# Low weight parts by accumulating transfer in a third of the up-projection chunks

## The chip, the core and the metric

The kernel runs on one core of one Trainium2 chip. The metric is the time of one execution on the device, in microseconds (us). The core has a matrix engine (TensorE, in the profile PE for its matmuls and PEld for its weight loads), a vector engine (VectorE, DVE), a scalar engine (ScalarE, ACT), a general engine (GpSimd, POOL) and an engine that issues transfers (SyncE, SP). Each works through its own queue in order, and the queues meet at semaphores. Sixteen DMA engines move data between the device's memory and the on-chip memory SBUF; matmul results go to PSUM.

## The reference

The computation is a trunk of two layers over 256 tokens of 2048 channels, in float32. Each layer has a token mixer and a gated channel mixer, each between two RMS norms and added to the residual:

```python
for i in range(DEPTH):
    h = rms_norm(x, p['mix_pre'])
    m = mixer_dilated_gqa(h, ...) if i % 2 == 0 else mixer_mla(h, ...)
    x = x + rms_norm(m, p['mix_post'])
    h = rms_norm(x, p['ffn_pre'])
    x = x + rms_norm(conv_glu(h, *p['ffn']), p['ffn_post'])

def conv_glu(h, w_up, conv_w, conv_b, w_down):
    u = h @ w_up                                   # 2048 x 11264
    gate, val = u[..., :D_FF], u[..., D_FF:]       # D_FF = 5632
    gate = depthwise_conv3(gate, conv_w, conv_b)
    return (gelu(gate) * val) @ w_down             # 5632 x 2048
```

The product `h @ w_up`, once per layer, is the up projection of this document.

## The kernel before

All weights are read from the device's memory once, in float32, as a single list of chunks of 128 x 1024 numbers (512 KB), in the order in which the matmuls use them. Four buffers named `raw` hold what has been loaded. The matmuls need float32 numbers in two parts: a high part `whi`, which is the weight rounded to the matrix engine's float32r type, and a low part `wlo`, what the rounding left over. I call making the two parts "parting" a chunk. `_split` does it: ScalarE casts `raw` to `whi` (line L173), then VectorE subtracts `whi` from `raw` into `wlo` (L174). There are three buffers of each part. Activations are parted in the same way (`xhl`, `gh`, `gl`).

`weights()` (L187) is called for every chunk just before its matmuls. It parts chunks up to two ahead of the one in use, so that three are parted at a time, and issues loads up to five ahead from SP's queue (L156). In the passages between the sub-layers (`lead` is set) it parts one ahead only.

An up projection has 22 groups of 512 columns, gate groups and value groups in turn; a group has 8 chunks, so a layer has 176. `proj_t` works through one group: the weights are the stationary operand, each chunk has 8 blocks of 128 x 128, and each block takes two matmuls, the high part against high and low activations (512 columns, L244) and the low part against the high activations (256 columns, L245). Four PSUM banks collect the group. Then ScalarE copies half of each bank (L305), VectorE adds the halves (L306), and the gate goes through convolution and GELU, the value through the product with the gate. The PSUM banks alternate between two sets, so the next group's matmuls run meanwhile.

The down projection, the mixers' projections and the output projections draw on the same list of chunks and the same buffers. In the down projection some chunks are sums of others (class `Seven`), made on VectorE.

The program gives each engine's instructions through a tile framework that puts each engine's queue in order when the program is built. The order isn't just that of the code: in the trace the cast of a later chunk stands between two copies of one evacuation. POOL issues nothing in this kernel.

Of the kernel before, what the change touches and what calls it, by code (L numbers as in the profile page):

```python
# [9 lines left out]
F32 = mybir.dt.float32  # L10
F32R = mybir.dt.float32r
BF16 = mybir.dt.bfloat16
AF = mybir.ActivationFunctionType
ALU = mybir.AluOpType
AX = mybir.AxisListType

P = 128
# [5 lines left out]
NFG = DFF // 512  # L23
HD = 128
EPS = 1e-6
NEG = -1e30
HOLD = 3
LAGS = 3, 2, 1

XM = 0, 1, 3, 2  # L30
# [7 lines left out]
def down_order(h):  # L38

    plain = [("plain", p, o) for o in range(2) for p in range(PAIRS, KF // 2)]  # L40
    out, plain = plain[:LEAD[h]], deque(plain[LEAD[h]:])
    for p in range(PAIRS):
        for j in (0, None, None, 1, None, 2, 3, None):
            out.append(plain.popleft() if j is None else ("seven", p, j))
    return out + list(plain)


class Seven:
# [5 lines left out]
    def __init__(self, a, b):  # L54
        self.srcs, self.raw = (a, b), None
# [31 lines left out]
class Model:  # L87
# [60 lines left out]
    def _load(self, i):  # L148
        if i >= len(self.chunks) or i in self.loaded or i < self.at or i in self.made:
            return  # L150
        if isinstance(self.chunks[i], tuple):
            self.chunks[i][0].load(self)
            self.loaded[i] = None
            return
        raw = self.wp.tile([P, 1024], F32, tag="raw", name="raw", bufs=4)
        self.nc.sync.dma_start(out=raw, in_=self.chunks[i])  # L156
        self.loaded[i] = raw

    def _split(self, i, parts=1):
        if i >= len(self.chunks) or i in self.made:  # L160
            return
        self._load(i)
        raw = self.loaded.pop(i)
        seven, step = self.chunks[i] if raw is None else (None, 0)
        if seven:
            raw = seven.step(self, step)
        hi = self.wp.tile([P, 1024], F32R, tag="whi", name="whi", bufs=3)
        lo = self.wp.tile([P, 1024], F32R, tag="wlo", name="wlo", bufs=3)
        n = raw.shape[-1] // parts
        with self.behind(self.gate):  # L170
            for j in range(parts):
                s = slice(n * j, n * j + n)
                self.nc.scalar.copy(hi[:, s], raw[:, s])  # L173
                self.nc.vector.tensor_tensor(out=lo[:, s], in0=raw[:, s], in1=hi[:, s].bitcast(F32),  # L174
                                             op=ALU.subtract)
        if seven and step == 0:
            seven.sums(self)
        self.made[i] = (hi, lo)
# [8 lines left out]
    def weights(self, upto=None):  # L187

        i = self.at
        if upto is None:  # L190
            upto = i + (2 if self.lead else 3)
            self.follow()
        for j in range(i, upto):
            self._split(j)
        for j in range(upto, i + 6):
            self._load(j) if j < upto + 4 else None
        self.at += 1
        return self.made.pop(i)
# [191 lines left out]
    def out_proj(self, nk, parts, post, pre, m3, order=None, before={}):  # L390
# [27 lines left out]
        part = self.three(ss)  # L418
        ps = self.proj_tok(nk, parts, order, hold=HOLD)
        m.append(room.tile([P, 2, 512], F32, tag=tag, name="m3", bufs=bufs))  # L420
# [103 lines left out]
    def attend(self, scores, sc, mask, v, v_gen, put, sp):  # L524
# [31 lines left out]
        for i in range(2):  # L556
            nc.vector.tensor_scalar(out=p[:, i, :], in0=p[:, i, :], scalar1=den[:, i:i + 1], scalar2=None,
                                    op0=ALU.mult)
        for _ in range(LAGS[0]):
            yield  # L560
# [9 lines left out]
        use["p"] -= 1  # L570
        for _ in range(LAGS[1]):
            yield
# [28 lines left out]
    def turned(self, sp, ps, n, block, tab, put, scale=None):  # L601
# [4 lines left out]
        for t in range(2):  # L606
# [25 lines left out]
            yield  # L632
        for _ in range(LAGS[2]):
            yield
# [367 lines left out]
    def down(self, gh, gl, post, pre):  # L1002
# [75 lines left out]
        ended = None  # L1078
        for h in range(2):
            items = down_order(h)  # L1080
            units = [n for n, item in enumerate(items) if item[0] == "seven"]
            if h == 0:
                gains.append(self.gain_row(post, 1))
            n = len(items) - (HOLD if h else 0)
            todo = [(i, t) for i in range(n) for t in range(2)] + \
# [9 lines left out]
            def products(i, t, w):  # L1095
                group = []
                while used and used[0][1][:2] == (i, t):
                    q, (_, _, b, x, blk) = used.popleft()
                    group.append((banks[b], *x(), slice(512 * blk, 512 * blk + 512), q == first[b], q == last[b]))
                for bank, xh, xl, c, start, _ in group:  # L1100
                    mm(bank, xh, w[0][:, c], start=start, stop=False)  # L1101
                    mm(bank, xl, w[0][:, c], start=False, stop=False)  # L1102
                for bank, xh, _, c, _, stop in group:
                    mm(bank, xh, w[1][:, c], start=False, stop=stop)  # L1104
# [22 lines left out]
        part = self.three(ss)  # L1127
        ws = [self.weights(self.at + HOLD - j) for j in range(HOLD)]
        for t in range(2):
            for j in range(HOLD):  # L1130
                products(n + j, t, ws[j])
# [24 lines left out]
    def all_chunks(self):  # L1156
        a = self.a
        groups = lambda w, gs: [w[g, c] for g in gs for c in range(w.shape[1])]
        out = groups(a["w_in0"], [8, 6, 7, 0, 2, 4, 1, 3, 5])
        out += [a["w_out0"][g, c] for g in range(4) for c in (4, 5, 6, 7, 0, 1, 2, 3)]  # L1160

        def down(w):
            items = []
            for h in range(2):
                pairs = [Seven(w[2 * h, p], w[2 * h + 1, p]) for p in range(PAIRS)]
                items += [w[2 * h + j, p] if kind == "plain" else (pairs[p], j) for kind, p, j in down_order(h)]
            return items

        ffn = lambda l: groups(a[f"w_up{l}"], [g for j in range(NFG) for g in (j, NFG + j)]) + \
            down(a[f"w_down{l}"])  # L1170
        out += ffn(0)
        out += groups(a["w_in1"], [0, 1]) + [a["w_kr"]]
        for p in range(8):
            out += groups(a["w_qr"], [p // 4]) if p % 4 == 0 else []
            out += [a["w_qn"][p], a["w_kn"][p]]
            out += groups(a["w_v"], [p // 2]) if p % 2 == 0 else []
        out += groups(a["w_out1"], range(4))
        out += ffn(1)
        return out
# [67 lines left out]
```

## Time and profile before

| | |
|---|---|
| time, median of 2 runs | 2062.1 us (2062.04 to 2062.15) |
| span of the profiled execution | 2060.1 us |
| time outside the span (median less span) | 2.0 us |
| PE, PEld, DVE, ACT, POOL busy | 99%, 85%, 72%, 55%, 0% of the span |
| first up projection | 331 to 820 us |
| second up projection | 1326 to 1818 us |
| moved in all | 385.96 MB, 187 GB/s on average |

The profiled execution has no time of its own on record beside its span; the 2.0 us is what the median of the timed runs has more.

In rows of groups, a line reads: line of the kernel, engine, operation, output and inputs with their shapes, count, then busy time in us and the mean of one in ns, then the idle time of the engine just before them and what ended it. In rows of waits: who waited, for whom, us in total, times, the longest. In rows of stretches: from and to in us, length, busy time of PE, PEld, DVE, ACT and POOL, the granted clock of TensorE (1.00 is full), the share of the DMA engines' time that was busy, and GB/s. In rows of a timeline: start, duration, instruction, and in brackets the idle time before. Matmuls are pipelined and their ends are modelled, so their busy times overlap.

### The profile page before, as it was taken

What the parts mean: (1) busy time and instruction counts of PE and PEld (TensorE: products, weight loads), DVE (VectorE), ACT (ScalarE), POOL (GpSimd) and SP (SyncE); (2) the same over time, 40 slices, a digit from 0 to 9 for tenths busy, and PEclk for the clock granted to TensorE, in tenths of its full rate; (3) what the DMA queues carried; (4) which work ended last, traced back from release to release, by engine and by line L of the source; (5) the groups of instructions that cost most, each with busy time, mean ns of one, the idle gap of its engine ahead of it and who ended that gap; (6) DMA issues with size and microseconds to landing.
All of it is one profiled execution on the core that took longest, in us unless ns stands there. A gap on an engine that the chain in (4) does not pass through costs nothing.

```text
span 2060.1 us, 29196 instructions
## 1 busy us (share of the span) xinstructions
PE 2043.4 (99%) x10905; PEld 1750.0 (85%) x10905; DVE 1478.4 (72%) x2263; ACT 1129.3 (55%) x1753; POOL 0.2 (0%) x4
## 2 busy tenths in 40 slices
PE   9999999999999999999999999999999999999998
PEld 7888888888888888888878998888888888888886
DVE  6877757766766767878787875676766766787877
ACT  6655546555555555555465664555555555554553
POOL 0000000000000000000000000000000000000000
PEclk9999999999999999999999999999999999999999
DMA  8545566666566666566655445566566566556664
GB/s 318 176 153 161 166 197 193 186 194 193 185 194 191 185 194 189 184 211 197 203 179 170 124 134 173 176 210 189 185 193 193 184 195 193 185 184 205 204 206 141
DMA packets 108717, 385.96 MB, mean 187 GB/s; under 512 B 12064, under 2 KB 12576, under 8 KB 108576
## 3 DMA queue, kind: packets, MB, share of 16 engines
q1 hardware_dynamic: 108288, 383.83, 59.3%
q8 instruction: 85, 1.39, 0.3%
q14 instruction: 56, 0.46, 0.1%
q10 hardware_dynamic: 288, 0.28, 0.0%
HBM read 381.96 MB, written 2.10 MB: 186 GB/s over the span
## 4 chain that ended last, share of the span: by engine, by line
PE 96%; DVE 3%; issue 0%; ACT 0%; DMA 0%; DVEq 0%; SPq 0%; ACTq 0%
PE ps L244 31%; PE ps L245 16%; PE ps L230 8%; PE ps L231 8%; PE ps L232 8%; PE ps L1104 7%; PE ps L1101 7%; PE ps L1102 7%; PE ps L537 1%; PE ps L300 1%; DVE x L454 1%; DVE wlo L174 1%; PE ps L478 0%; DVE sums L1005 0%; DMA raw<-in_w_in 0%
## 5 line engine op out<-in xcount | busy, mean ns | idle before, releaser
L174 DVE TENSOR_TENSOR wlo<-raw,whi 128x1024 fp32r<-128x1024 f32 (+1 forms) x662 | 807.6, 1221 | 490.3 <-ACT whi L173 487.6
L173 ACT CAST whi<-raw 128x1024 fp32r<-128x1024 f32 (+1 forms) x662 | 694.3, 1050 | 642.7 <-PE ps L244 302.4
L244 PE MATMUL ps<-xhl,whi 128*128 128x512 f32 x2816 | 978.7, 394 | 1.0 <-DVE xhl L591 1.0
L245 PE MATMUL ps<-xhl,wlo 128*128 128x256 f32 x2816 | 779.2, 277 | 0.0
L244 PEld LDWEIGHTS ps<-xhl,whi 128*128 128x128 f32 x2816 | 527.6, 188 | 123.1 <-DVE xhl L591 2.0
L245 PEld LDWEIGHTS ps<-xhl,wlo 128*128 128x128 f32 x2816 | 528.9, 188 | 1.0 <-DVE wlo L174 0.5
L1101 PE MATMUL ps<-whi,gh 128*128 128x512 f32 x584 | 227.3, 389 | 0.0
L1102 PE MATMUL ps<-whi,gl 128*128 128x512 f32 x584 | 227.2, 389 | 0.0
L1104 PE MATMUL ps<-wlo,gh 128*128 128x512 f32 x584 | 182.0, 390 | 0.8 <-DVE wlo L174 0.8
L230 PE MATMUL ps<-whi,xhl 128*128 128x512 f32 x352 | 138.7, 395 | 0.9 <-ACT whi L173 0.8
L231 PE MATMUL ps<-wlo,xhl 128*128 128x512 f32 x352 | 137.6, 391 | 0.0
L232 PE MATMUL ps<-whi,xhl 128*128 128x512 f32 x352 | 137.2, 390 | 0.0
L1104 PEld LDWEIGHTS ps<-wlo,gh 128*128 128x128 f32 x584 | 109.1, 188 | 25.2 <-DVE wlo L174 2.7
L1101 PEld LDWEIGHTS ps<-whi,gh 128*128 128x128 f32 x584 | 109.6, 188 | 22.8
L1102 PEld LDWEIGHTS ps<-whi,gl 128*128 128x128 f32 x584 | 109.6, 188 | 22.8
L230 PE MATMUL ps<-whi,oh 128*128 128x512 f32 x256 | 100.0, 390 | 0.0
L231 PE MATMUL ps<-wlo,oh 128*128 128x512 f32 x256 | 99.7, 389 | 0.0
L232 PE MATMUL ps<-whi,ol 128*128 128x512 f32 x256 | 99.6, 389 | 0.0
L305 ACT COPY half<-ps 128x256 f32<-128x256 f32 x176 | 65.1, 370 | 43.9 <-PE ps L244 34.6
L230 PEld LDWEIGHTS ps<-whi,xhl 128*128 128x128 f32 x352 | 66.0, 188 | 14.5 <-ACT whi L173 1.1
L232 PEld LDWEIGHTS ps<-whi,xhl 128*128 128x128 f32 x352 | 66.1, 188 | 13.9
L231 PEld LDWEIGHTS ps<-wlo,xhl 128*128 128x128 f32 x352 | 66.3, 188 | 13.4 <-DVE wlo L174 0.9
(211 smaller groups left out, 2061.0 us busy)
## 6 DMA issues: line engine op xcount, KB each, us to landing
raw<-in_w_up SPq DMA_DIRECT2D x352, 512.0 KB, 4.1
raw<-in_w_down SPq DMA_DIRECT2D x128, 512.0 KB, 3.9
raw<-in_w_in SPq DMA_DIRECT2D x88, 512.0 KB, 3.7
raw<-in_w_out SPq DMA_DIRECT2D x64, 512.0 KB, 4.1
seven_a<-in_w_down SPq DMA_DIRECT2D x24, 512.0 KB, 4.5
seven_b<-in_w_down SPq DMA_DIRECT2D x24, 512.0 KB, 4.2
gb<-in_post SPq DMA_DIRECT2D x16, 256.0 KB, 3.8
raw<-in_w_qn SPq DMA_DIRECT2D x8, 512.0 KB, 3.6
```

The lines of the kernel that those rows point to most:

```text
L173: self.nc.scalar.copy(hi[:, s], raw[:, s])
L174: self.nc.vector.tensor_tensor(out=lo[:, s], in0=raw[:, s], in1=hi[:, s].bitcast(F32), op=ALU.subtract)
L230: mm(ps, lh, rh, start=start, stop=False)
L231: mm(ps, lh, rl, start=False, stop=False)
L232: mm(ps, ll, rh, start=False, stop=stop)
L244: mm(out[i], hi[:, s], x(k), start=k == 0, stop=False)
L245: mm(out[i][:, :T], lo[:, s], x(k)[:, :T], start=False, stop=k == nk - 1)
L300: self.tc.keep_in_program_order(self.nc.tensor.transpose(out, x, self.ident))
L305: self.nc.scalar.copy(b, ps[:, T:])
L1101: mm(bank, xh, w[0][:, c], start=start, stop=False)
L1102: mm(bank, xl, w[0][:, c], start=False, stop=False)
L1104: mm(bank, xh, w[1][:, c], start=False, stop=stop)
```

## The change

Three things change.

First, in both up projections every third chunk from number 8 of the layer on (8, 11, 14, ...) is wrapped in a new class `Summed`. For such a chunk ScalarE casts `raw` to `whi` as before and then also writes the negated high part into `wlo`. VectorE does nothing. A transfer issued from POOL's queue reads the same 512 KB of weights from the device's memory a second time and adds them, on the way, to what lies in `wlo`: the low part is weight minus high part, as before. All other chunks are parted as before.

Second, `whi` and `wlo` get four buffers instead of three, and `weights()` parts up to three chunks ahead instead of two, for all chunks of the kernel. Loads still reach up to five ahead.

Third, the scratch memory that the program reserves in SBUF for the descriptors of transfers issued from POOL is set to 1024 bytes per partition.

```diff
+AHEAD = 4
+class Summed:
+    def __init__(self, src):
+        self.src = src
     def _load(self, i):
         raw = self.wp.tile([P, 1024], F32, tag="raw", name="raw", bufs=4)
-        self.nc.sync.dma_start(out=raw, in_=self.chunks[i])
+        src = self.chunks[i]
+        self.nc.sync.dma_start(out=raw, in_=src.src if isinstance(src, Summed) else src)
     def _split(self, i, parts=1):
-        hi = self.wp.tile([P, 1024], F32R, tag="whi", name="whi", bufs=3)
-        lo = self.wp.tile([P, 1024], F32R, tag="wlo", name="wlo", bufs=3)
+        hi = self.wp.tile([P, 1024], F32R, tag="whi", name="whi", bufs=AHEAD)
+        lo = self.wp.tile([P, 1024], F32R, tag="wlo", name="wlo", bufs=AHEAD)
         n = raw.shape[-1] // parts
+        if isinstance(self.chunks[i], Summed):
+            with self.behind(self.gate):
+                self.nc.scalar.copy(hi, raw)
+                self.nc.scalar.activation(lo, hi.bitcast(F32), AF.Copy, scale=-1.0)
+            self.nc.gpsimd.dma_start(out=lo, in_=self.chunks[i].src, accum_op=ALU.add)
+            self.made[i] = (hi, lo)
+            return
     def weights(self, upto=None):
-            upto = i + (2 if self.lead else 3)
+            upto = i + (2 if self.lead else AHEAD)
...
-        ffn = lambda l: groups(a[f"w_up{l}"], [g for j in range(NFG) for g in (j, NFG + j)]) + \
-            down(a[f"w_down{l}"])
+        def up(w):
+            items = groups(w, [g for j in range(NFG) for g in (j, NFG + j)])
+            return [Summed(src) if i % 3 == 2 and i >= 8 else src for i, src in enumerate(items)]
+        ffn = lambda l: up(a[f"w_up{l}"]) + down(a[f"w_down{l}"])
...
-    nc = bacc.Bacc("TRN2", target_bir_lowering=False, num_devices=1)
+    nc = bacc.Bacc("TRN2", target_bir_lowering=False, num_devices=1,
+                   dynamic_dma_scratch_size=1024)
```

## The prediction

> **What bounds the kernel now.** I read the busy times first, then the chain of work that ended last, then who waited for whom inside the up projections, where the change acts.
>
> ```profile
> PE 2043.4 (99%) x10905; PEld 1750.0 (85%) x10905; DVE 1478.4 (72%) x2263; ACT 1129.3 (55%) x1753; POOL 0.2 (0%) x4
> ...
> PE 96%; DVE 3%; issue 0%; ACT 0%; DMA 0%; DVEq 0%; SPq 0%; ACTq 0%
> ```
>
> TensorE is busy for 2043.4 of 2060.1 us and makes up 96% of the chain. So 16.7 us, 0.8% of the span, is all that any change to other engines could win if TensorE's work stays as it is. POOL does next to nothing. The stages of the change come next (start and end in us; then busy time of PE, PEld, DVE, ACT and POOL, granted clock, DMA share, GB/s): the two up projections, and a third row from the kernel's start, where transfers run as fast as they ever do here.
>
> ```profile
> 331.00:820.00 489.00, 488.52 (x2824) 426.88 (x2823) 340.24 (x542) 271.56 (x419) 0.00 (x0) 1.00 0.62 191
> 1326.00:1818.00 492.00, 491.51 (x2840) 429.40 (x2840) 343.12 (x548) 274.26 (x423) 0.00 (x0) 1.00 0.62 191
> ...
> 10.00:15.00 5.00, 5.00 (x22) 3.81 (x22) 4.83 (x9) 4.59 (x7) 0.00 (x0) 1.00 1.04 417
> ```
>
> In 981 us of up projection TensorE idles for 1.0 us, at full clock. VectorE works 70% of that time and ScalarE 56%, both with room. The waits of the weight loads in the first of these stages say the same: they waited for a low part (wlo) once.
>
> ```profile
> PEld ps L244 <- DVE xhl L591: 1.0, 2, 0.8
> PEld ps L245 <- DVE wlo L174: 0.2, 1, 0.2
> ```
>
> So the VectorE work that the change takes away is off the path, and its removal is worth nothing by itself. The question is whether what replaces it arrives in time. A steady stretch of ScalarE shows the beat (start, duration, then in brackets the idle time before and who ended it):
>
> ```profile
> 456.76 1.05 ACT L173 CAST whi<-raw 128x1024 fp32r<-128x1024 f32 x1 [1.46 <-PE ps L244]
> 459.53 1.05 ACT L173 CAST whi<-raw 128x1024 fp32r<-128x1024 f32 x1 [1.72 <-PE ps L244]
> 462.30 1.05 ACT L173 CAST whi<-raw 128x1024 fp32r<-128x1024 f32 x1 [1.72 <-PE ps L244]
> 465.08 1.05 ACT L173 CAST whi<-raw 128x1024 fp32r<-128x1024 f32 x1 [1.72 <-PE ps L244]
> ```
>
> One chunk of weights takes TensorE 2.77 us. Each cast waits for the end of the matmuls that free its buffer: with three buffers that is the chunk three before, and the cast has two chunks, 5.5 us, until its own chunk's matmuls start.
>
> **The change, part by part.** 176 chunks make one up projection. Those with a remainder of 2 by three from number 8 on are 8, 11, ..., 173: 56 per layer, 112 in all.
>
> *Removed from VectorE:* 112 subtractions. *Added to ScalarE:* 112 negations of 128x1024. Both prices stand in the groups:
>
> ```profile
> L174 DVE TENSOR_TENSOR wlo<-raw,whi 128x1024 fp32r<-128x1024 f32 (+1 forms) x662 | 807.6, 1221 | 490.3 <-ACT whi L173 487.6
> L173 ACT CAST whi<-raw 128x1024 fp32r<-128x1024 f32 (+1 forms) x662 | 694.3, 1050 | 642.7 <-PE ps L244 302.4
> ```
>
> VectorE loses 112 x 1.22 = 137 us, ScalarE gains 112 x 1.05 = 118 us (I price the negation as the cast: same size, both out of SBUF). On the path: 0 for both. The negation is covered by the 1.72 us in which ScalarE idles before the next cast; without that cover each would push the next cast by 1.05 us, which has a slack of 8.3 - 2.3 us.
>
> *Added transfers:* 112 of 512 KB on POOL's queue, each adding weights to what lies in SBUF. POOL has nothing else queued, so its wait for the negation holds up nobody; behind the transfer stand the 16 low-part matmuls of that chunk, and behind the first of them all of TensorE's queue, high-part matmuls of the same chunk included. No such transfer is in the trace, so I bound it by the plain loads of the same size:
>
> ```profile
> L156 SPq DMA_DIRECT2D raw<-in_w_up x171: 327/328/328, 334.9 to 807.3; - x171
> ...
> DMA to landing us min/median/max: 3.2/4.1/5.4
> ```
>
> A plain load lands 3.2 to 5.4 us after its issue, 4.1 as a rule. At 417 GB/s 512 KB take 1.26 us, so 3.2 - 1.26 = 1.94 us lie around the moving, issue included. The accumulating one must also read what is in SBUF. From below it costs no more than the quickest load, 3.2 us. From above I take the slowest load, two further passes of the bytes (the reading back, and as much again for adding or queueing), and one whole 1.94 us more for an issue by POOL: 5.4 + 2.52 + 1.94 = 9.9 us. My value is 4.1 + 1.26 + 0.5 = 5.9 us: the median load, one more pass, and an issue dearer by a quarter of the 1.94, since it is nearest to the plain load of the same bytes over the same engines.
>
> The Trainium skill, in "Collectives: The Full Stack", section "The bandwidth ceiling: the fold count and why AG ≠ RS ≠ AR", says that the add in the transfer engines costs its two source reads and no cycles of its own. "DMA: Bandwidth & Descriptors", section "Specifications", puts the first byte of a software-issued transfer at about 1 us against 0.6 us for a hardware-issued one. By these two the transfer would be estimated at 4.1 + 1.26 + 0.4 = 5.8 us and the run would come out with my forecast; no run here shows either yet.
>
> *Moved: the lead.* With four buffers the parting of a chunk starts when the chunk four before it ends and must be done three chunks later, 3 x 2.77 = 8.3 us. Cast and negation take 2.1 us, hand-overs some 0.1. That leaves 6.1 us for the transfer, against 5.9 wanted: on time with 0.2 us to spare. Let C be the whole chain, 2.2 us plus the transfer. If C exceeds 8.3, TensorE stalls; but the chain of the next such chunk, three later, starts before that stall and gains from it, so two neighbours share C - 8.3, and the mean stall is half of it.
>
> At the ends of groups ScalarE is behind, because it evacuates PSUM in between:
>
> ```profile
> 442.89 1.05 ACT L173 CAST whi<-raw 128x1024 fp32r<-128x1024 f32 x1 [1.72 <-PE ps L244]
> 443.84 0.37 ACT L305 COPY half<-ps 128x256 f32<-128x256 f32 x1
> ...
> 445.89 1.06 ACT L173 CAST whi<-raw 128x1024 fp32r<-128x1024 f32 x1
> ...
> 451.83 1.04 ACT L173 CAST whi<-raw 128x1024 fp32r<-128x1024 f32 x1
> ```
>
> By the beat these casts were due at 445.66 and 451.20, so they come 0.2 and 0.6 us late, and with another 1.05 us of ScalarE in the same stretch up to 1.6. About four chunks of sixteen lie there, 28 of the 112. Taking 0.8 us of lateness, less 0.2 spare, halved: 28 x 0.3 = 8 us. Ends: 0 (the planner moves the evacuation) and 28 x 0.8 = 22 us.
>
> *Raw loads and their queue.* They run one fewer ahead of the parting, but parting itself is one further ahead, so the horizon of six chunks stays. SP's loads wait for a raw buffer as before:
>
> ```profile
> SPq L156 <- DVE wlo L174: 1229.2, 518, 9.2
> ```
>
> A buffer comes free 2.3 us after a parting starts (cast plus subtraction), and the load into it is cast four chunks after that start: 11.1 - 2.3 - 4.1 = 4.7 us of slack before and after. For summed chunks ScalarE alone frees it, 1.2 us sooner. If an accumulating transfer pushes a load by its whole two passes, 2.5 us, it stays inside 4.7. Cost 0; without that cover a load would stall TensorE by what exceeds it.
>
> *Transfer engines.* 191 GB/s in the stage plus a third of it at two passes is 191 x (1 + 2/3) = 318 GB/s, 76% of 417. At three passes 382 (92%), at four 446, more than there is.
>
> *The fourth buffer elsewhere.* At the two passages into the up projections one parting stands in the chain, between residual additions:
>
> ```profile
> 325.53 1.41 DVE x L454 x2
> 326.94 1.14 DVE wlo L174
> ...
> 1322.17 1.14 DVE wlo L174
> ```
>
> With a free buffer it can be done before: between 0 and 2 x 1.14 = 2.3 us won; I take 2, near the upper end, since the cast of that chunk then no longer waits for the last matmuls to free its buffer. The scratch is cut from what nothing in the kernel used so far; 0.
>
> *The sum,* against the profiled execution: 2060.1 + 0 + 8 - 2 = 2066.1 us of span, and the 2.0 us that the median of 2062.1 lies above the span: 2068 us, 0.3% above before. What this kernel's measurement can tell from no change I take as 2%, 41 us.
>
> **The rivals.**
>
> *Late transfers (slower).* Mechanism: the accumulating transfer outlasts the lead. Place: the first low-part matmul of 112 chunks. It decides from a transfer of 6.1 us on, and passes 2% at a mean stall of about 0.3 us beside the 8 us of the group ends, that is from 6.7 us on. At 4.1 + 1.26 + 1.94 = 7.3 us, the full price for POOL's issue, C is 9.5 and the sum is 112 x 0.59 = 66 us, less the 2, plus 8: 2134 us. At the upper bound, 9.9 us, it is 112 x 1.9 = 213 us, 2281 us. For it: the spare of 0.2 us is far less than what I don't know of the issue and of queueing beside loads that already fill 62% of the engines' time. Against it: plain loads at that share land within 5.4 us. Chance 0.35.
>
> *Transfers become the bound (slower).* If adding costs four passes, 446 of 417 GB/s: at least 7% of 981 us, 69 us; and by latency 4.1 + 3 x 1.26 + 0.5 = 8.4 us, C = 10.6, 112 x 1.15 = 129 us with the group ends beside it: 2062 + 129 + 6 = 2197 us. For it: nothing in the trace; against it: 24% of the speed is free at two passes. Chance 0.07.
>
> *Faster by over 2%.* TensorE's 16.7 us of idling would have to vanish two and a half times over. Less work on VectorE could matter only if TensorE itself ran slower beside it, and the clock is 1.00 in these stages. 2 us from the passages: 2060. Chance 0.01.
>
> That the change doesn't do what it says I leave out: its edits name the chunks outright.
>
> **The numbers.** Forecast (on time, with small stalls at most): 0.57, own range 2057 to 2103. Late transfers 0.35, bound by transfers 0.07, faster 0.01. The predicted time is the forecast's, 2068. The range goes from 2057 (both gains, no stalls, a little below) to 2160, which takes in two thirds of the late case; left out are its upper third, 0.12, most of the 0.07 and the 0.01. Faster by over 2% 0.01, within 2% 0.57, slower 0.42.
>
> **What would show it.** The waits of L245's weight loads: some 10 us in all for the forecast, 60 and more in the name of the POOL transfer if it is late, in alternate summed chunks. The median from issue to landing of the new transfers: below 6.1 us or above. VectorE's busy time near 1341 us, ScalarE's near 1247, 58.7 MB more moved (112 x 0.524), a DMA share in the up stages between 0.75 and 0.9 (over 1.0 for the third case). The raw loads landing in under 8 us. The forecast is wrong if the transfer takes over 6.7 us, if POOL's issue alone takes over 1 us and adds to the landing time, or if the negations, by the order on ScalarE, come later than right behind their cast.

## The result and the profile after

The changed kernel takes 2175.5 us (median of 2 runs, 2172.7 to 2178.2) against 2062.1 before: a ratio of 1.053, 95% interval 1.050 to 1.057 (the two medians alone would give 1.055). It is 113 us slower by the medians, 110 by the ratio, and lies above the stated range. The profiled execution has a span of 2171.0 us, 110.9 more than before.

The page of the changed kernel: busy times, the two transfer queues (q1 is SP's, q0 the new one from POOL; packets, MB, share of the sixteen engines' span) and the chain that ended last.

```profile
PE 2076.5 (96%) x10905; PEld 1763.7 (81%) x10905; DVE 1358.6 (63%) x2151; ACT 1236.1 (57%) x1865; POOL 97.8 (5%) x116
...
q1 hardware_dynamic: 108288, 383.83, 54.5%
q0 software_dynamic: 16128, 58.73, 16.5%
...
PE 63%; issue 20%; DMA 11%; DVE 3%; POOL 2%; ACT 1%; POOLq 0%; DVEq 0%; SPq 0%; ACTq 0%
```

VectorE's busy time fell by 120 us and ScalarE's rose by 107, a little less than the 137 and 118 that were worked out: VectorE's subtractions did lose 137 us (807.6 to 670.2) and the negations do take 118.7, but the rest of VectorE's busy time rose by 17 us, and that of ScalarE fell by 12. The chain, 96% TensorE before, now runs for 11% through DMA and for a fifth through "issue", which is time in which the engine waited for nothing that the profile shows. So I read the cause from the waits. The waits of TensorE's low-part instructions are these (L260 is the old L245; L182 is the new transfer):

```profile
PEld ps L260 <- DMA wlo<-in_w_up: 101.3, 76, 3.5
PE ps L260 <- DMA wlo<-in_w_up: 77.5, 64, 3.2
```

The new transfer's own line (durations of its issue on POOL in ns, least, median, most; then its landing):

```profile
L182 POOL DMA_DIRECT2D wlo<-in_w_up x112: 862/866/1007, 351.6 to 1913.9; - x112
...
DMA to landing us min/median/max: 5.4/7.3/9.2
```

Before, these weight loads waited for a low part once in each up projection, for 0.2 and 0.3 us. Now TensorE waits for the transfers in most of the 112 summed chunks. (The two rows can't be added: a weight load's wait and its matmul's overlap.) The transfer takes POOL 0.87 us to issue and lands 7.3 us after its issue, where a plain load took 4.1. On TensorE's timeline one stall looks like this:

```profile
459.92 0.39 PE L259 MATMUL ps<-xhl,whi 128*128 128x512 f32 x1
461.58 0.39 PE L260 MATMUL ps<-xhl,wlo 128*128 128x256 f32 x1 [1.27 <-DMA wlo<-in_w_up]
461.81 0.39 PE L259 MATMUL ps<-xhl,whi 128*128 128x512 f32 x1
```

The low-part matmul should have started some 0.23 us after the high-part one, as in the blocks behind it; it started 1.66 us after it. And this is the path of the same chunk that set the time, first on ScalarE, then on POOL:

```profile
451.53 1.05 ACT L180 CAST whi<-raw 128x1024 fp32r<-128x1024 f32 x1 [1.72 <-PE ps L259]
452.61 1.06 ACT L181 ACTIVATE wlo<-whi 128x1024 fp32r<-128x1024 f32 x1
```

```profile
454.07 0.88 POOL L182 DMA_DIRECT2D wlo<-in_w_up  x1 [8.45 <-ACT wlo L181]
```

From the start of the cast to POOL's issue are 2.54 us, and a transfer lands 7.3 us after that in the median: a chain of 9.8 us against a lead of 8.3.

### The profile page after: what moved, and what is told of

It is laid out like the page before. It is cut to its first block, busy times and chain, and to the rows that moved or that the text cites. A ratio compares the mean times of both kernels' runs of the same rounds, so it can differ in the third digit from the quotient of the medians.

```text
span 2171.0 us, 29553 instructions
## 1 busy us (share of the span) xinstructions
PE 2076.5 (96%) x10905; PEld 1763.7 (81%) x10905; DVE 1358.6 (63%) x2151; ACT 1236.1 (57%) x1865; POOL 97.8 (5%) x116
## 3 DMA queue, kind: packets, MB, share of 16 engines
q0 software_dynamic: 16128, 58.73, 16.5%
## 4 chain that ended last, share of the span: by engine, by line
PE 63%; issue 20%; DMA 11%; DVE 3%; POOL 2%; ACT 1%; POOLq 0%; DVEq 0%; SPq 0%; ACTq 0%
DMA wlo<-in_w_up 11%; PE ps L259 10%; PE ps L245 8%; PE ps L246 8%; PE ps L247 8%; PE ps L1116 7%; PE ps L1117 7%; PE ps L1119 7%; PE ps L260 6%; POOL wlo L182 2%; PE ps L552 1%; PE ps L315 1%; DVE wlo L189 1%; DVE x L469 1%; DMA raw<-in_w_up 0%
## 5 line engine op out<-in xcount | busy, mean ns | idle before, releaser
L189 DVE TENSOR_TENSOR wlo<-raw,whi 128x1024 fp32r<-128x1024 f32 (+1 forms) x550 | 670.2, 1221 | 618.1 <-ACT whi L188 615.2
L259 PE MATMUL ps<-xhl,whi 128*128 128x512 f32 x2816 | 995.9, 397 | 1.7 <-DVE xhl L606 1.7
L260 PE MATMUL ps<-xhl,wlo 128*128 128x256 f32 x2816 | 800.0, 284 | 77.9 <-DMA wlo<-in_w_up 77.5
L188 ACT CAST whi<-raw 128x1024 fp32r<-128x1024 f32 (+1 forms) x550 | 574.3, 1050 | 495.2 <-PE ps L259 250.8
L260 PEld LDWEIGHTS ps<-xhl,wlo 128*128 128x128 f32 x2816 | 535.3, 190 | 102.0 <-DMA wlo<-in_w_up 101.3
L180 ACT CAST whi<-raw 128x1024 fp32r<-128x1024 f32 x112 | 117.4, 1049 | 130.3 <-PE ps L259 127.3
L182 POOL DMA_DIRECT2D wlo<-in_w_up x112 | 97.6, 872 | 1816.7 <-ACT xhl L605 538.7
L245 PE MATMUL ps<-whi,xhl 128*128 128x512 f32 x352 | 138.8, 396 | 1.4 <-ACT whi L188 1.1
L181 ACT ACTIVATE wlo<-whi 128x1024 fp32r<-128x1024 f32 x112 | 118.7, 1060 | 2.2
L188 ACT CAST whi<-seven_a 128x1024 fp32r<-128x1024 f32 x48 | 50.6, 1054 | 103.1 <-PE ps L1117 86.4
L245 PE MATMUL ps<-whi,oh 128*128 128x512 f32 x256 | 100.0, 390 | 0.0
```

The costliest lines, as they stand in the source:

```text
L181: self.nc.scalar.activation(lo, hi.bitcast(F32), AF.Copy, scale=-1.0)
L182: self.nc.gpsimd.dma_start(out=lo, in_=self.chunks[i].src, accum_op=ALU.add)
L245: mm(ps, lh, rh, start=start, stop=False)
L259: mm(out[i], hi[:, s], x(k), start=k == 0, stop=False)
L260: mm(out[i][:, :T], lo[:, s], x(k)[:, :T], start=False, stop=k == nk - 1)
```

## The experiments

Two theories stood against each other after the result. **A, late transfers:** each transfer outlasts the lead, and what counts is the length of the chain against the lead. **B, taken speed:** 58.7 MB more through the engines, at double cost, slow everything, and what counts is the bytes. Ratios are to the kernel before on the same chip, with 95% intervals. The runs of the kernel before lie at 2062, 2071 or 2080 us, in steps of 9, so differences under half a per cent are left to the intervals.

**One chunk more of lead** (`lead_four`).

```diff
-AHEAD = 4
+AHEAD = 5
```

> The changed kernel with five buffers of each part and parting four chunks ahead; all else as changed. Theory A (late transfers): the chain of a summed chunk, cast, negation, hand-over and transfer, is 1.05 + 1.06 + 0.4 + 7.3 = 9.8 us in the changed kernel's profile, against a lead of 3 x 2.77 = 8.3. With 4 x 2.77 = 11.1 us of lead it fits but for the slowest (the longest landing is 9.2 us, chain 11.7), so nearly all of the 113 us go: 2062 to 2072 us. Theory B (the transfers take speed from everything: two passes of a third of the weights, contention with the loads): the bytes are the same, so the time stays above 2150 us.

Ratio 1.005 (1.003 to 1.008); the profiled execution takes 2071.5 us, the median of ten runs is 2078.6, which is a little above the 2062 to 2072 expected. The transfers are as slow as before; they only start a chunk earlier (landing, then TensorE's waits):

```profile
DMA to landing us min/median/max: 5.3/7.3/10.2
```

```profile
PEld ps L260 <- DMA wlo<-in_w_up: 6.2, 9, 1.7
PE ps L260 <- DMA wlo<-in_w_up: 3.7, 5, 1.4
```

Same bytes, same landing, and some 100 of the 110 us are gone. B is refuted as the main cause, A holds.

**One chunk less of lead** (`lead_two`): `AHEAD = 3`.

> The changed kernel with three buffers of each part as before, parting two chunks ahead; the third of the chunks still gets its low part by transfer. Theory A: the lead is 2 x 2.77 = 5.5 us, the chain 9.8 to 10.3, and the parting of the next summed chunk starts only after the stall of this one, so nothing is shared: 4.3 to 4.8 us of stall at each of 112 chunks, 480 to 540 us more than before, 2540 to 2600 us. Theory B: same bytes, same time as changed, about 2175 us.

Ratio 1.190 (1.186 to 1.194), 2461.5 us: 391 us more than before by the ratio, not 480 to 540. All 112 weight loads wait, up to 4.9 us.

```profile
PEld ps L260 <- DMA wlo<-in_w_up: 318.3, 112, 4.9
```

The span and the mean granted clock of the core:

```profile
core 0: 2461.5 us, clock 0.960
```

The expectation took 7.3 us for the landing. Here TensorE stands still for so long that fewer plain loads move beside the transfer: while one moves, 42 packets of plain loads start in the median, where 124 do in the changed kernel. It lands in 5.7 us: chain 2.5 + 5.7 = 8.2, less 5.5 of lead, 112 x 2.7 = 302 us. The rest is in the second row: the mean granted clock fell from 0.998 to 0.960, and by estimate that is 0.038 x 2461 = 94 us. Together 396.

**Half as many transfers** (`sixth`).

```diff
-            return [Summed(src) if i % 3 == 2 and i >= 8 else src for i, src in enumerate(items)]
+            return [Summed(src) if i % 6 == 2 and i >= 8 else src for i, src in enumerate(items)]
```

> The changed kernel with every sixth chunk summed (8, 14, 20, ...) instead of every third: 56 transfers instead of 112. Theory A with shared stalls: neighbours six apart no longer overlap, so each stalls for the whole of chain less lead, 1.5 to 2.0 us, instead of half of it: 56 x 1.5 to 2.0 = 84 to 112 us, so 2146 to 2174 us, little less than with twice as many transfers. Theory A without sharing: half of 113 us, 2119 us. Theory B: half the extra bytes, half the loss or less, at most 2119 us.

Ratio 1.035 (1.030 to 1.040): about 72 us for 56 transfers, 1.29 us each, where the changed kernel pays 110 us for 112, 0.98 each. Halving the transfers doesn't halve the loss (55 us), so neighbours three chunks apart do share a stall. The waits say the same:

```profile
PEld ps L260 <- DMA wlo<-in_w_up: 73.0, 51, 2.3
```

Here 51 of 56 weight loads wait, in the changed kernel 76 of 112. Over the first nine summed chunks of the changed kernel TensorE's timeline has low-part matmuls late by 2.4, 0, 0, 1.8, 0, 1.6, 0, 2.2 and 0 us: a late chunk is mostly followed by one on time. With sharing in full the sixth would have lost 84 us or more by the expectation, and 56 x (2.54 + 7.2 - 3 x 2.77) = 80 us by its own landing. It lost some 72, below the expected range, and the changed kernel more than half of a full stall for each chunk. So sharing is there, and somewhat weaker than the formula says.

**The negation ahead of the cast** (`neg_first`).

```diff
-                self.nc.scalar.copy(hi, raw)
-                self.nc.scalar.activation(lo, hi.bitcast(F32), AF.Copy, scale=-1.0)
+                self.nc.scalar.activation(lo, raw, AF.Copy, scale=-1.0)
+                self.nc.scalar.copy(hi, raw)
```

> The changed kernel with the two ScalarE instructions of a summed chunk exchanged: the negation is made from the raw weights, rounded in the same way, ahead of the cast. The transfer can then be issued 1.05 us sooner. Theory A: chain shorter by 1.05 us, mean stall shorter by half of it, 112 x 0.53 = 59 us: 2116 us. Theory B: 2175 us, nothing moves. Without sharing: 1.0 us off each stall, near 2062 us.

Ratio 1.064 (1.061 to 1.068): slower than the changed kernel, a miss. ScalarE's timeline shows that the edit didn't do what I wanted. The order of the queue was set when the program was built, and it put the cast first all the same in 92 of the 112 chunks:

```profile
446.83 1.05 ACT L181 CAST whi<-raw 128x1024 fp32r<-128x1024 f32 x1 [1.77 <-PE ps L259]
447.79 1.05 ACT L180 ACTIVATE wlo<-raw 128x1024 fp32r<-128x1024 f32 x1
```

So it says nothing on the length of the chain. But it is worse than the changed kernel, by more than 20 us, and it lands in 7.8 us instead of 7.3. Why, the next runs show.

**The negation on VectorE, beside the cast** (`neg_vector`).

```diff
+                self.nc.vector.tensor_scalar(out=lo, in0=raw, scalar1=-1.0, scalar2=None, op0=ALU.mult)
                 self.nc.scalar.copy(hi, raw)
-                self.nc.scalar.activation(lo, hi.bitcast(F32), AF.Copy, scale=-1.0)
```

> The changed kernel with the negation made by VectorE straight from the raw weights, beside ScalarE's cast. VectorE idles for 1.5 us before each parting in the steady stretches. Theory A: the chain is the negation (0.6 to 1.2 us, no row yet) and 7.7 us, 8.3 to 8.9, so stalls of 0 to 0.3 us on average and some at the ends of groups: 2065 to 2105 us. Theory B: 2175 us. A third possibility is that VectorE's work holds up POOL's issue, which would show as an issue longer than 0.87 us.

Ratio 1.053 (1.045 to 1.061): nothing gained, though the negation takes 0.69 us on VectorE and POOL issues 1.2 us after the cast's start instead of 2.54. POOL's issue is still 0.87 us, so the third possibility falls. The landing ate the gain:

```profile
DMA to landing us min/median/max: 7.1/8.0/9.8
```

The packets of the queues in the trace say where. Medians in us, worked out from each transfer's first and last packet and from the last issue of a load by SP before it; the third column is the sum of the first two:

```
kernel            after SP's load   issue to 1st packet   load's issue to 1st packet   1st to last   landing
changed                1.47               1.65                      3.1                  5.2          7.3
lead_two               1.47               1.61                      3.1                  3.7          5.7
no_add                 1.47               1.66                      3.1                  2.9          4.9
neg_first              0.38               2.54                      2.9                  4.9          7.8
half_columns           0.32               2.64                      3.0                  2.9          5.9
neg_vector             0.15               3.00                      3.2                  4.6          8.0
neg_vector_hold        0.15               3.03                      3.2                  4.6          8.1
```

With SP's load 1.4 us or more ahead, the first packet comes 1.6 to 1.7 us after POOL's issue. With the load less than 0.4 us ahead, in the last four rows, it comes 2.5 to 3.0 us after it, which is again some 3 us after the load's issue. In the kernel before, a load that is alone starts to move 1.0 us after its issue and has moved after about 3.2. So the transfer seems to start behind that load (theory C), and the load is one that the parting itself sets off, by freeing a raw buffer.

**Holding the raw buffer back** (`neg_vector_hold`): ScalarE reads the raw weights once more, in two halves, into a scrap tile, behind the transfer's issue.

```diff
             self.nc.gpsimd.dma_start(out=lo, in_=self.chunks[i].src, accum_op=ALU.add)
+            junk = self.small.tile([P, 512], BF16, tag="junk", name="junk", bufs=1)
+            for s in (slice(0, 512), slice(512, 1024)):
+                self.nc.scalar.copy(junk, raw[:, s])
```

> As neg_vector (negation on VectorE beside the cast), and ScalarE reads the raw weights of a summed chunk once more behind the cast, into a scrap tile that nobody uses, so that the raw buffer comes free some 1.2 us later and the plain load that waits for it is issued after the accumulating transfer instead of just before it. In neg_vector the chain was 1.3 us shorter than changed up to the issue, but the transfer's first packet came 3.0 us after its issue instead of 1.65 and nothing was won. Theory C (the transfer starts behind the load that its own cast releases): first packet back to about 1.7 us, landing about 6.7 to 7.0 instead of 8.0, chain 8.0 to 8.3 against a lead of 8.3: stalls only at the ends of groups, 2070 to 2105 us. Rival D (an early issue is slow for another reason, VectorE's work beside POOL's, say): landing stays at 8.0 us, 2165 to 2185 us.

Ratio 1.061 (1.055 to 1.066), inconclusive: SP still issued a load 0.15 us before each transfer, as the table shows, so the load that I meant to move hadn't moved. It doesn't decide between C and rival D of its expectation, by which the early issue is slow for another reason, such as VectorE's work beside POOL's.

**That load behind the transfer, in POOL's queue** (`neg_vector_pool_load`), on top of `neg_vector`:

```diff
-        self.nc.sync.dma_start(out=raw, in_=src.src if isinstance(src, Summed) else src)
+        queue = self.nc.gpsimd if i > 3 and isinstance(self.chunks[i - 4], Summed) else self.nc.sync
+        queue.dma_start(out=raw, in_=src.src if isinstance(src, Summed) else src)
```

> As neg_vector, and the plain load into the raw buffer that a summed chunk frees (the chunk four later) is issued from POOL's queue instead of SP's, where it stands behind that chunk's accumulating transfer. In neg_vector SP issued a load 0.15 us before each accumulating transfer, whose first packet then came 3.0 us after its issue; in the kernels where the last load lay 1.47 us back it came after 1.65 us. Theory C (the transfer starts only when the load issued just before it has moved): first packet back to 1.6 to 1.8 us, landing at most 7.0 us instead of 8.0, chain 1.2 + 7.0 = 8.2 us against a lead of 8.3, stalls at the ends of groups alone: 2068 to 2105 us. Rival D (VectorE's negation beside POOL's issue, or the early issue as such, delays it): first packet stays at 3.0 us, 2165 to 2190 us.

Ratio 1.014 (1.007 to 1.020), 2093.6 us, within what C expected. The first packet is back at 1.58 us after the issue, SP's last load lies 1.68 us back, and the landing is the shortest of all kernels that move 512 KB by adding beside a running TensorE:

```profile
DMA to landing us min/median/max: 5.2/6.3/7.9
```

```profile
PEld ps L261 <- DMA wlo<-in_w_up: 23.6, 38, 1.6
PE ps L261 <- DMA wlo<-in_w_up: 11.7, 25, 1.3
```

VectorE's negation and the early issue are as in `neg_vector`, so D falls. C holds, and A with it: the chain is now 1.2 + 6.3 = 7.5 us, under the lead, and the waits shrink to a quarter or less.

**Writing without adding** (`no_add`).

```diff
-            self.nc.gpsimd.dma_start(out=lo, in_=self.chunks[i].src, accum_op=ALU.add)
+            self.nc.gpsimd.dma_start(out=lo, in_=self.chunks[i].src)
```

> The changed kernel with the same transfers from POOL's queue, at the same places, that only write the weights into the low part and add nothing (the low part is then the whole weight, so the products differ from the reference). It removes the reading back of what lies in the buffer and keeps POOL's issue, the change of type and the hand-over. If the second read is what made the transfer dear: busy time of the transfers' packets from 16.5% of the engines' span to about 8 to 9%, landing from 7.3 to about 5.7 us, chain 8.2 us, stalls nearly gone: 2065 to 2085 us. If POOL's issue or the change of type is: landing stays near 7 us, time above 2150 us.

Ratio 1.006 (1.003 to 1.008). Its rows, packets of both queues, POOL's issue, the landing and TensorE's waits:

```profile
q1 hardware_dynamic: 108288, 383.83, 57.4%
q0 software_dynamic: 16128, 58.73, 9.0%
```

```profile
L182 POOL DMA_DIRECT2D wlo<-in_w_up x112: 527/530/662, 352.4 to 1818.6; - x112
...
DMA to landing us min/median/max: 4.0/4.9/6.3
...
PEld ps L260 <- DMA wlo<-in_w_up: 1.8, 4, 0.6
```

Same bytes, same queue, same change of type: without the adding the packets take 9.0% of the engines' span instead of 16.5%. A single packet of 4 KB takes 174 ns instead of 328 (medians; 159 on SP's queue). The landing falls by 2.4 us, and the stalls are gone. Of the 2.4 us 2.3 lie between the first packet and the last (5.2 and 2.9 in the table); that POOL's issue is shorter by 0.34 us doesn't bring the first packet forward. The Trainium skill, "Collectives: The Full Stack", section "The bandwidth ceiling: the fold count and why AG ≠ RS ≠ AR", puts the price of an add at two source reads; the 328 against 174 ns agree with that.

**Half the columns by transfer** (`half_columns`): in a summed chunk, VectorE subtracts the first 512 columns, and negation and transfer cover the other 512.

```diff
-                self.nc.scalar.activation(lo, hi.bitcast(F32), AF.Copy, scale=-1.0)
-            self.nc.gpsimd.dma_start(out=lo, in_=self.chunks[i].src, accum_op=ALU.add)
+                self.nc.scalar.activation(lo[:, 512:], hi[:, 512:].bitcast(F32), AF.Copy, scale=-1.0)
+                self.nc.vector.tensor_tensor(out=lo[:, :512], in0=raw[:, :512], in1=hi[:, :512].bitcast(F32),
+                                             op=ALU.subtract)
+            self.nc.gpsimd.dma_start(out=lo[:, 512:], in_=self.chunks[i].src[:, 512:], accum_op=ALU.add)
```

> The changed kernel, but in a summed chunk only the second 512 of the 1024 columns get their low part by transfer (256 KB), the first 512 by VectorE's subtraction. Theory A with a transfer that has a fixed part of about 4 us and 3.2 us for 512 KB: landing about 5.7 us, negation 0.55 instead of 1.06, chain 7.7 us, under the lead of 8.3: 2062 to 2075 us. If the transfer's time were all in its issue and completion: landing near 7 us, chain 9.0, 112 x 0.35 = 39 us, 2101 us.

Ratio 1.005 (1.003 to 1.008): as A expects (the median, 2076.6 us, is 2 us above the expected range). 256 KB land in 5.9 us, move for 2.9, and start late behind a load (2.64 us).

**Twice the scratch** (`scratch_2k`): 2048 bytes instead of 1024.

> The changed kernel with 2048 instead of 1024 bytes of scratch per partition for the descriptors of POOL's transfers. If the small scratch made POOL or the transfer engines wait, landing drops below 7.3 us and the time below 2150 us. If not, which the 0.87 us of every issue speaks for, it stays at 2170 to 2180 us.

Ratio 1.051 (1.045 to 1.057), landing 7.4 us: the scratch isn't what makes the transfer slow.

**The lead alone, and the scratch alone** (`lead_only`: no chunk is summed; `scratch_only`: the kernel before with 1024 bytes of scratch).

> The changed kernel without any summed chunk: four buffers of each part, parting three ahead, small scratch, all low parts made by VectorE. Prediction's term: 0 to 2.3 us won at the passages, 2059 to 2062 us. lead_four, no_add and half_columns all came out 0.5% above before without late transfers; in their profiles a pair of up-projection matmuls takes 348 to 351 ns on average instead of 347. If the transfers beside the matmuls do that, this kernel stays at 2062 us or below; if the place of the buffers or the order of the instructions does, it shows the same 0.3 to 0.5% (2068 to 2072 us).

> The kernel before with nothing changed but the scratch of 1024 bytes per partition. It moves all tiles to other places in SBUF and changes nothing else. If the place in SBUF slows the matmul pairs, it shows some of the 0.3 to 0.5%; else 2062 us as before.

Ratios 1.001 (0.999 to 1.004) and 1.001 (0.999 to 1.003). The second is from eleven of its twelve runs; the twelfth took 5292 us, and nothing on record says why. Neither part costs or wins anything that can be told. The profiled execution of `lead_only` took 2071.6 us, one step of 9 above the kernel before, without any transfer from POOL, and its pairs of up-projection matmuls take 350.1 ns on average instead of 346.9 (from start to start, longer pauses left out): 2816 x 3.2 ns = 9 us. In `lead_four`, `no_add` and `half_columns` they take 348.3 to 351.3 ns, so the half per cent of these three is at least in part the same lengthening. No version beat the kernel before.

## Why the prediction was wrong

*What bounds the kernel:* right. VectorE's 137 us were off the path, ScalarE's 118 pushed no later cast into TensorE's way (with a longer lead, in `lead_four`, they cost next to nothing), though the negation is a link of the late chain. The raw loads stayed harmless (landing 4.6 us in the median), the engines' share in the stages rose to 0.84 (0.75 to 0.9 expected), and the passages' 2 us can't be told from none.

*The mechanism of the loss:* named, as the rival with 0.35, with its place and its point of decision. Its signs came out: the waits of over 60 us in the transfer's name, a landing above 6.1 us, and late chunks that mostly alternate with punctual ones. A transfer of 7.3 us was even the example worked out there, but that this figure agrees is luck: the example got it by charging a full 1.94 us for POOL's issue, and the runs put the excess elsewhere. The forecast chose 5.9.

*The step that failed* is the price of the accumulating transfer, "the median load, one more pass, and an issue dearer by a quarter of the 1.94". The issue's 0.5 us was right: without adding, the transfer lands in 4.9 us, beside plain loads of 4.4 us in the same run. The pass was mis-sized. I took 1.26 us for it, at the rate of the fastest stretch of the kernel. It costs 7.3 - 4.9 = 2.4 us. In the packets' own time the price was about right: 128 packets over sixteen engines are 8 each, if they are spread evenly, and 8 x (328 - 174) ns = 1.2 us. But a transfer that moves for longer shares the engines with more of the plain loads. In the changed kernel the 18 transfers during which fewer than 50 packets of plain loads started moved in 3.8 us, the 57 with 120 to 200 such packets in 5.4 (medians). With the engines already busy for 0.62 of the time, the peak rate was the wrong price for the pass.

*The rival's sum* was too low as well, 2134 us at 7.3. Of the 41 us that are missing, 112 x 0.17 = 19 are the hand-over from ScalarE to POOL: cast to issue is 2.54 us, where I had 2.2. Another 7 are the clock, below. Of the remaining 15, some 7 are pairs of up-projection matmuls that take 349.4 ns instead of 346.9, away from stalls and from half clock (2816 x 2.5 ns). What is left lies in the ends of groups and a sharing weaker than half; I haven't separated them.

*Halving by neighbours:* it was borne out in kind (0.98 us each against 1.29 each alone), not in full.

*The range* ended at 2160 because it left out the upper third of the late case. With 2.4 us for the pass the transfer would have come to 7.0 us, and the prediction's own formula to 112 x 0.45 = 50 us: 2118 us, in the late case, and still short of what was measured.

One reading was wrong without effect: a chunk has 8 low-part matmuls, not 16, and no term was worked out from that.

## What to carry to other kernels

Before moving work from an engine that isn't on the path to a transfer, hold the whole chain against the lead: every hand-over, the issue, the moving at the share that the engines already carry, and what is issued just ahead. Here VectorE's work wasn't on the path, so taking it away won nothing, and the transfer that replaced it could only cost. One more buffer of lead won the time back nearly whole (110 us to some 10), while shortening one link (`neg_vector`) only moved the wait into the next.

## What the runs showed of the hardware

**Waiting costs clock.** TensorE's clock is granted in stretches: the changed kernel has five at half speed, each one or two times 3.41 us long or at the end of the run, where the kernel before has only the one at its end. One of them, and the stretches before and after it (granted clock third from the right):

```profile
551.20:554.60 3.40, 1.64 (x9) 1.28 (x9) 0.23 (x1) 1.59 (x3) 0.00 (x0) 1.00 0.98 329
554.60:558.00 3.40, 3.40 (x13) 2.81 (x12) 2.34 (x6) 2.59 (x7) 0.89 (x1) 0.50 0.66 175
558.00:561.40 3.40, 3.40 (x21) 3.02 (x20) 3.35 (x7) 2.79 (x5) 0.00 (x0) 1.00 0.64 120
```

In the first, TensorE was busy for 1.64 of 3.40 us; in the second it got half its clock though it had work throughout. The four stretches at half speed within the changed kernel's run came each after a stretch of 3.41 us in which TensorE was busy for 0.16, 0.35, 0.39 and 0.48 of the time; the idlest such stretches that weren't followed by one had 0.48 and 0.50. In `sixth`, with stalls of up to 2.3 us, but no such stretch under 0.51, the clock stayed whole until the end. So in these traces it is the busy share of such a stretch, at about a half, that goes with the loss, and not the length of one wait. By estimate it costs (0.998 - 0.995) x 2171 = 7 us in the changed kernel, and 94 in `lead_two`. The Trainium skill, "TensorE: Matmul & The Clock Gate", section "What's actually happening", gives a window of 3413 ns that runs on its own, and half the clock after an idle one; the length agrees with the trace, while the stretches before the loss weren't idle here but busy for up to 0.48. Its rule of no idle gaps beyond some 3 us, in "Why this matters for your kernels", is too mild for this kernel: the longest single wait around this stretch was 2.1 us, and the clock fell all the same.

**A transfer starts behind the load issued just before it on another queue.** In the four kernels where POOL issued 0.15 to 0.38 us behind the load, the first packet came 2.5 to 3.0 us after POOL's issue, 2.9 to 3.2 after the load's; with the load 1.47 us ahead, or moved behind the transfer, 1.6 to 1.7 us after POOL's issue. Whether the engines or the making of descriptors cause it stays open.

**Steps of 9 us** in the kernel before (2062, 2071, 2080) occur without any of the change's parts. The one profile that shows such a step without any transfer from POOL, of `lead_only`, has pairs of matmuls that are 1% longer on average; no profile of the kernel before was taken on a step, and what causes them wasn't tried.
